# All gates as Strassen sets ahead of a dilated attention without fill

## The chip, the cores and the metric

The kernel runs on one core of a Trainium2 chip. The metric is the device time of one execution in microseconds, as the median of several runs; lower is better. TensorE (PE) multiplies matrices into PSUM, VectorE (DVE), ScalarE (ACT) and GpSimd (POOL) work elementwise, and SyncE (SP) issues most of the DMA transfers. Each engine runs its own queue in order and waits on semaphores of the others.

## What is computed

One encoder layer is applied to a sample of 1024 rows and a prompt of 256 rows with shared weights, all in float32. Cut to what matters here:

```python
h = rmsnorm(x, norm1_g) * (1 + sc1) + sh1
z = einsum('bsd,de->bse', h, w_in)
c_q, c_kv, k_r, qkv_d, gate_a, gate_b = split(z, cuts)
o_a = mla_attention(...)                      # 16 heads, from c_q, c_kv, k_r
...
# dilated attention: 3 groups of 4 heads of 64, (window, dilation) = (128,1), (512,4), (2048,16)
s = einsum('bqhd,bqjhd->bhqj', q_b, k_g) * scale + alibi
lse = logsumexp(s); p = exp(s - lse)
o = einsum('bhqj,bqjhd->bqhd', p, v_g)
...
o_b = sum(softmax(lses over groups) * outs)
merged = sigmoid(gate_a) * (o_a @ p_a) + sigmoid(gate_b) * (o_b @ p_b)
x = x + gt1 * (merged @ w_out)
```

A conv feed-forward block and a last norm follow.

## The kernel before

A float32 product is made of three products of float32r operands: each operand is split into a high part and the rest, and high x high, high x low and low x high are summed in PSUM (`mm3`, line 88, and its generator `mm3_steps`, line 95). T is 1280 columns (sample and prompt), in chunks `CH` of 512, 512 and 256. All activations lie transposed, 128 features by T.

The first 392 us make the normed input `hH`, `hL` and project it. `product_set` (line 290) multiplies two blocks of 128 output features by a Strassen scheme: seven products of 24 matmuls of 320 columns (`product`, line 235) and sums of them on VectorE and GpSimd. The list `psets` holds ten such sets: queries and keys of the dilated attention (`qk_d`), four blocks of gate b (`gb_d`) and four latent blocks (`lt_d`).

Then comes the dilated attention. Six steps (three groups, two pairs of heads) go over ten tiles of 128 query rows each. `queries_keys` loads a pair's queries and keys from `qk_d` (two heads on 128 partitions), copies the high part on ScalarE (line 628) and subtracts on VectorE (line 630); group 2 is not split. `weights` makes the scores (line 890) for two heads in two PSUM banks, a biased minimum on VectorE (line 895) and the exponential on ScalarE (line 900). `outputs` transposes them on PE (line 910), copies them out of PSUM (lines 914, 916, 919), multiplies by the values (line 925) and copies the result (lines 929, 931).

Between these pieces a fill is issued: `filler` runs 13 blocks (one latent block, four of gate b, eight of gate a), each as 72 plain matmuls by `block` and `mm3_steps` (line 99), 19 pieces for every 20 half tiles (`SIDE`). Beside it run `norms` (the latents' norms) and `modulation` (the second half of the adaLN projection, line 770, with its 256 KB weight loads). What is left of the fill after the last step runs together with `merge`, the combination of the second pair. The first pair is combined in the last step. Then `latents`, `ropes`, `values_out` and `branch_b` follow (gate b, the product with `p_b`), and then the latent attention.

The order on each engine is set by a scheduler of the tile framework from the order in which the code issues the work; buffers (`bufs`) bound how far it can run ahead.

## Time and profile before

| | us |
|---|---|
| median of 3 runs (2441.15 to 2444.96) | 2443.45 |
| the profiled execution | 2446.51 |
| its span | 2444.7 |

| stage, us from the start | what runs |
|---|---|
| 0 to 147 | norm, modulation, first values |
| 147 to 392 | ten Strassen sets |
| 392 to 413 | fill, loads of the first step |
| 413 to 698.5 | dilated attention and fill |
| 698.5 to 743 | rest of the fill, second combination |
| 743 to 809 | ropes, branch B |
| after 809 | latent attention, output, feed-forward |

A row of the windows view gives a stretch's length and each engine's busy time in it, with the number of instructions; PEclk is the granted TensorE clock as a share of 2.4 GHz, and the DMA share is the mean busy share of the 16 DMA engines. PE counts as busy from a matmul's start to its modelled end. A timeline row is start, length, engine, line, operation, output <- input and count; PEld is the weight load.

### The profile page before, as it was taken

The numbers are of one execution on the slowest core, as the hardware profiler recorded it, in microseconds if no ns is written. First come the engines' busy times: TensorE is split into PE (matmuls) and PEld (weight loads), VectorE is DVE, ScalarE is ACT, GpSimd is POOL, SyncE is SP. The second block draws the span as 40 slices with busy tenths as digits, with TensorE's granted clock in tenths as the row PEclk, the third lists the DMA queues.
The fourth block names the chain that finished last, engine by engine and source line by source line (L and its number), as shares of the span: only waits on it lengthen the run. The fifth ranks groups of instructions, "written<-read, shape, count | busy, mean of one in ns | idle before, by whom it ended". The sixth has DMA issues, their size and how long they took to land. (4 is left out here: it accounts for less than half of the span.)

```text
span 2444.7 us, 36879 instructions
## 1 busy us (share of the span) xinstructions
PE 2345.5 (96%) x13115; PEld 1990.2 (81%) x13115; DVE 1508.4 (62%) x2526; ACT 1078.3 (44%) x2102; POOL 1033.7 (42%) x758
## 2 busy tenths in 40 slices
PE   7999999999999999999998999989999999999987
PEld 3899997666677777777776788789999999988875
DVE  4743333443458688888897533486655665559678
ACT  4421212554434477777776433353222322343434
POOL 1033331100135166666677441004655565439373
PEclk9999999999999999999999999999999999999998
DMA  7232225567458833333332853332322223177554
GB/s 266 74 115 97 98 82 181 185 196 237 152 156 291 280 86 85 87 86 88 89 109 74 227 178 118 124 121 78 110 95 81 82 95 105 56 267 241 174 185 153
DMA packets 208019, 342.48 MB, mean 140 GB/s; under 512 B 24365, under 2 KB 86686, under 8 KB 207834
## 3 DMA queue, kind: packets, MB, share of 16 engines
q1 hardware_dynamic: 182238, 311.00, 39.7%
q10 hardware_dynamic: 25596, 29.12, 3.4%
q8 instruction: 103, 1.69, 0.3%
q14 instruction: 82, 0.67, 0.1%
HBM read 236.67 MB, written 94.19 MB: 135 GB/s over the span
## 5 line engine op out<-in xcount | busy, mean ns | idle before, releaser
L243 PE MATMUL X<-t,wh 128*128 128x320 f32 x2864 | 537.3, 309 | 6.9 <-ACT ut L1777 6.9
L243 PEld LDWEIGHTS X<-t,wh 128*128 128x128 f32 x2864 | 450.6, 188 | 7.2 <-ACT ut L1777 7.1
L80 POOL TENSOR_TENSOR pl<-p,ph 128x512 fp32r<-128x512 f32 x224 | 298.4, 1342 | 135.4 <-ACT ph L1190 102.0
L243 PE MATMUL X<-t,wl 128*128 128x320 f32 x1432 | 327.1, 310 | 1.9 <-DVE wl L77 1.0
L243 PEld LDWEIGHTS X<-t,wl 128*128 128x128 f32 x1432 | 239.6, 188 | 3.0 <-DVE wl L77 1.6
L1189 ACT ACTIVATE p<-S 128x512 f32<-128x512 f32 x272 | 163.5, 601 | 105.4 <-issue 39.6
L1171 DVE TENSOR_REDUCE m<-mi 128x1 f32<-128x512 f32 x256 | 174.0, 686 | 35.7 <-PE mi L1170 32.8
L229 ACT CAST wh<-wr 128x512 fp32r<-128x512 f32 x113 | 70.2, 622 | 280.7 <-PE X L243 183.2
L99 PE MATMUL pp<-t,wh 128*128 128x512 f32 (+1 forms) x624 | 188.3, 381 | 0.5 <-DVE sm L663 0.5
L77 DVE TENSOR_TENSOR ut<-X,ut 128x640 f32<-128x640 f32 x126 | 101.5, 819 | 130.7 <-PE X L243 78.2
L1190 ACT ACTIVATE ph<-S 128x512 fp32r<-128x512 f32 x272 | 162.6, 598 | 1.2 <-issue 0.4
L1869 PE MATMUL Y<-bh,ah 128*128 128x512 f32 x385 | 151.8, 395 | 8.2 <-DVE ut L77 6.8
L80 POOL TENSOR_TENSOR wl<-R,wh 128x512 fp32r<-128x512 f32 x60 | 96.4, 1607 | 146.0 <-ACT wh L229 146.0
L1869 PE MATMUL Y<-bl,ah 128*128 128x512 f32 x385 | 151.9, 395 | 6.2 <-POOL bl L80 6.2
L1869 PE MATMUL Y<-bh,al 128*128 128x512 f32 x385 | 151.4, 393 | 0.0
L80 POOL TENSOR_TENSOR wl<-wr,wh 128x512 fp32r<-128x512 f32 (+2 forms) x39 | 45.4, 1165 | 247.1 <-ACT wh L208 216.3
L77 DVE TENSOR_TENSOR wl<-wr,wh 128x512 fp32r<-128x512 f32 x128 | 112.8, 883 | 48.1 <-ACT wh L229 41.7
L243 PE MATMUL X<-R,wh 128*128 128x320 f32 x736 | 138.1, 309 | 0.0
L99 PEld LDWEIGHTS pp<-t,wh 128*128 128x128 f32 x624 | 107.4, 192 | 30.4 <-issue 12.7
L77 DVE TENSOR_TENSOR pt<-X,pt 128x640 f32<-128x640 f32 x60 | 48.6, 823 | 134.8 <-PE X L243 83.8
L77 DVE TENSOR_TENSOR al<-ar,ah 128x640 fp32r<-128x640 f32 x75 | 93.6, 1249 | 55.8 <-ACT ah L1843 55.8
L77 DVE TENSOR_TENSOR ac<-ac,p 128x512 f32<-128x512 f32 x160 | 111.0, 694 | 9.2 <-ACT p L1189 7.1
(436 smaller groups left out, 5668.9 us busy)
## 6 DMA issues: line engine op xcount, KB each, us to landing
ac_d<-ut SPq DMA_DIRECT2D x77, 320.0 KB
ar<-ac_d SPq DMA_DIRECT2D x75, 320.0 KB
R<-in_w_up_dram SPq DMA_DIRECT2D x84, 256.0 KB
br<-in_w_down_dram SPq DMA_DIRECT2D x77, 256.0 KB
ad<-in_ada_w_dram SPq DMA_DIRECT2D x64, 256.0 KB
rw<-in_w_in_dram SPq DMA_DIRECT2D x20, 512.0 KB
V<-v_d SPq DMA_DIRECT2D x16, 640.0 KB
v<-in_ada_w_dram SPq DMA_DIRECT2D x32, 256.0 KB
```

What stands on the lines that cost most here:

```text
L77: nc.vector.tensor_tensor(out=out, in0=a, in1=b, op=op)
L80: nc.gpsimd.tensor_tensor(out=out, in0=a, in1=b, op=op)
L99: nc.tensor.matmul(ps, lhsT=w[k], rhs=x[k], start=(k == 0 and w is wh and x is xh), stop=(k == n - 1 and w is wl))
L229: nc.scalar.copy(out=h, in_=a)
L243: nc.tensor.matmul(ps[:, z, 0:320], lhsT=a[:, k, :], rhs=b[q][k][:, 320 * z:320 * z + 320], start=(j == 0 and i == 0), stop=(j == n - 1 an ...
L1171: nc.vector.reduce_max(out=m2[:, i, c:c + 1], in_=ps, axis=AX.X)
L1189: nc.scalar.activation(out=p_, in_=ps, func=AF.Exp, scale=MSCALE)
L1190: nc.scalar.activation(out=ph, in_=ps, func=AF.Exp, scale=MSCALE)
L1869: nc.tensor.matmul(ps, lhsT=a[:, P * j:P * j + P], rhs=b, start=(f == 0 and a is ah and b is bh), stop=(f == HF - 1 and a is al))
```

## The change

All 16 gate blocks are now Strassen sets: `psets` holds the queries and keys, the latents, gate b and gate a, 16 sets. The one latent block left over is made plain after the eighth set by `lone_block`. The fill is gone (`filler`, `block`, `SIDE`), and with it `hH`, `hL`, whose pool is closed ahead of the attention.

A head's keys are now stacked: the high part on partitions 0 to 63, the low part on 64 to 127. The queries stand twice, as high parts and as low parts. So two products of 128 rows a head give all four terms, and group 2 is split as well. Each query and key piece is fetched twice, to both halves. The keys' copy is made on GpSimd.

Scores of a tile lie in one PSUM bank of three for two heads, and are issued two tiles ahead (`AHEAD`), across steps. Results of groups 0 and 1 go to DRAM (`nt_d`) and are read back by `combine`. The second combination is moved behind the attention, beside ropes and latents; branch B begins after it.

```diff
-    GB0 = 4
-    psets += [(B_GB + 2 * i, gb_d[2 * i:2 * i + 2]) for i in range(GB0 // 2)]
     psets += [(B_KV, lt_d[3:5]), (0, lt_d[0:2])]
+    psets += [(B_GB + 2 * i, gb_d[2 * i:2 * i + 2]) for i in range(KD // 2)]
+    psets += [(B_GA + 2 * i, ga_d[2 * i:2 * i + 2]) for i in range(KD // 2)]
+    def lone_block(b, to):
+        w = load_w(wpl, w_in[b], P, 4, WB)
+        xs_ = [X() for _ in range(2)]
+        for c, (c0, n) in enumerate(CH):
+            mm3(xs_[c // 2][:, c % 2, 0:n], *w, [t[:, c0:c0 + n] for t in hH], [t[:, c0:c0 + n] for t in hL])
...
-    w0 = load_w(wpl, w_in[2], P, 4, WB)
+        if i == 7:
+            lone_block(2, lt_d[2])
...
-    VB, SB = 8, 7
+    VB, SB, RB, PPB, AHEAD = 10, 9, 14, 1, 2
+    close_pool(hcm)
...
+        for h in range(2):
+            hs = slice(64 * h, 64 * h + 64)
+            kk, qh, ql = [rtile(F32R) for _ in range(3)]
+            res.append((kk, qh, ql))
+            for w, dh in ((1, kk), (0, qh)):
+                for c, (c0, n) in enumerate(CH):
+                    raw = qkt()[:, 0:n]
+                    for z in range(2):
+                        nc.sync.dma_start(out=raw[64 * z:64 * z + 64], in_=qk_d[g, w, pair, hs, c0:c0 + n])
+                    src = natural(raw, g, c)
+                    if w:
+                        nc.gpsimd.tensor_copy(by_class(dh, g, c), src)
+                    else:
+                        nc.scalar.copy(out=by_class(dh, g, c), in_=src)
+                    if w:
+                        dve_tt(by_class(kk[64:P], g, c), natural(raw[64:P], g, c), by_class(f32(kk[64:P]), g, c), ALU.subtract)
+                    else:
+                        dve_tt(by_class(ql, g, c), src, by_class(f32(qh), g, c), ALU.subtract)
+                    yield
...
-            terms = ((qh, kh), (qh, kl), (ql, kh)) if split else ((qh, kh),)
-            for t, (a, b_) in enumerate(terms):
-                for h in range(2):
-                    hs = slice(64 * h, 64 * h + 64)
-                    nc.tensor.matmul(ps[h][:, 0:wn], lhsT=a[hs, q0:q0 + P], rhs=b_[hs, w0:w0 + wn], start=(t == 0), stop=(t == len(terms) - 1))
+            ps = bank("S", 3)
+            for h, (kk, qh, ql) in enumerate(self.heads):
+                for t, a in enumerate((qh, ql)):
+                    nc.tensor.matmul(ps[:, 256 * h:256 * h + wn], lhsT=a[:, P * i:P * i + P], rhs=kk[:, w0:w0 + wn], start=(t == 0), stop=(t == 1))
...
+                nc.sync.dma_start(out=nt_d[pair, g], in_=self.nt)
...
     merge1 = merge()
-    for j, _ in enumerate(side):
-        if j % 4 == 1 or j < 4:
-            next(merge1, None)
-    run(merge1)
+    next(merge1)
...
     for _ in range(12):
         next(rr, None)
-        next(bb, None)
+        next(merge1, None)
         next(lat, None)
+    run(merge1)
```

PE in the middle of the attention, before (group 1 of the first pair, not its start). `PT` and `O` are the banks of the transposed weights and of the outputs, `pp` is the fill's:

```order
L99 MATMUL pp_4452<-t_135,wl_4289 128x512
L910 MATMUL PT_4500<-t_60,sm_4423 128x128 x4
L99 MATMUL pp_4452<-t_136,wh_4294 128x512
L99 MATMUL pp_4452<-t_144,wh_4294 128x512
L99 MATMUL pp_4452<-t_136,wl_4295 128x512
L99 MATMUL pp_4452<-t_137,wh_4294 128x512
L925 MATMUL O_4507<-sm_4501,v_3698 64x128 x4
L99 MATMUL pp_4452<-t_145,wh_4294 128x512
L99 MATMUL pp_4452<-t_137,wl_4295 128x512
```

The same engine at the change of a step, in the changed kernel:

```order
L913 MATMUL O_6279<-sm_6273,v_5652 64x128 x4
L898 MATMUL PT_6353<-t_60,sm_6267 128x128 x4
L879 MATMUL S_6370<-R_5682,R_5683 128x256
L879 MATMUL S_6370<-R_5682,R_5684 128x256
L879 MATMUL S_6370<-R_5819,R_5820 128x256
L879 MATMUL S_6370<-R_5819,R_5821 128x256
L879 MATMUL S_6415<-R_6102,R_6103 128x256
L879 MATMUL S_6415<-R_6102,R_6104 128x256
L879 MATMUL S_6415<-R_6231,R_6232 128x256
L879 MATMUL S_6415<-R_6231,R_6233 128x256
L770 MATMUL AD_6295<-ad_6296,t_104 32x512
L913 MATMUL O_6319<-sm_6313,v_5652 64x128 x4
```

Fill matmuls stood between the transpositions of a tile and its outputs; now scores of later tiles (the second four are of the next step) and transpositions of a later tile stand there, and here and there a modulation matmul (`AD`).

SP's queue at the end of the Strassen stage, before (`pt` is a set's output, `v` a value tile, `qk` a raw query or key piece):

```order
L560 DMA lt_d<-pt_3455 128x1280
L615 DMA v_3695<-vn_d 64x256
L615 DMA v_3695<-vn_d 128x256
L615 DMA v_3698<-vn_d 128x256 x2
L615 DMA v_3701<-vn_d 128x256 x2
L615 DMA v_3704<-vn_d 128x256 x2
L615 DMA v_3707<-vn_d 64x256
L615 DMA v_3707<-vn_d 128x256
L615 DMA v_3710<-vn_d 128x256
L626 DMA qk_3714<-qk_d 128x512
L626 DMA qk_3718<-qk_d 128x512
L626 DMA qk_3722<-qk_d 128x256
```

And in the changed kernel:

```order
L573 DMA ga_d<-pt_4899 128x1280
L630 DMA v_5128<-vn_d 64x256
L630 DMA v_5128<-vn_d 128x256
L630 DMA v_5131<-vn_d 128x256 x2
L630 DMA v_5134<-vn_d 128x256 x2
L630 DMA v_5137<-vn_d 128x256 x2
L630 DMA v_5140<-vn_d 64x256
L630 DMA v_5140<-vn_d 128x256
L630 DMA v_5143<-vn_d 128x256
L643 DMA qk_5148<-qk_d 64x512 x2
L643 DMA qk_5153<-qk_d 64x512 x2
L643 DMA qk_5158<-qk_d 64x256 x2
```

The queue has the same order, the last set's outputs first; the pieces of queries and keys are halves now, 24 of them for the first step where six stood.

## Rows read from the trace of the kernel before

**Rows 1.** Windows by stage: length, each engine's busy time (instructions), clock, DMA

```profile
core 0: us, PE busy (x) PEld busy (x) DVE busy (x) ACT busy (x) POOL busy (x), PEclk, DMA share, GB/s
147.00:392.00 245.00, 245.00 (x1672) 245.00 (x1672) 83.85 (x109) 49.45 (x81) 86.59 (x67) 1.00 0.26 95
...
392.00:413.00 21.00, 19.32 (x96) 15.23 (x95) 3.88 (x6) 4.39 (x8) 2.57 (x2) 1.00 0.81 267
413.00:698.50 285.50, 275.59 (x1715) 182.92 (x1713) 127.11 (x446) 139.07 (x396) 33.31 (x27) 0.98 0.59 187
698.50:743.00 44.50, 44.20 (x237) 37.99 (x237) 21.61 (x31) 12.51 (x21) 11.54 (x6) 1.00 0.69 209
743.00:809.00 66.00, 61.37 (x325) 52.07 (x325) 55.26 (x98) 31.63 (x68) 36.37 (x30) 0.97 0.91 306
```

**Rows 2.** The same windows, the fill's matmuls (line 99) alone: PE, PEld

```profile
413.00:698.50 285.50, 162.35 (x616) 100.49 (x614) 0.98 0.59 187
698.50:743.00 44.50, 44.09 (x236) 37.96 (x236) 1.00 0.69 209
```

**Rows 3.** Timeline of PE, fill alone: start, length, what, count

```profile
395.92 0.62 PE L99 MATMUL pp<-t,wh 128*128 128x512 f32 x2
396.38 0.39 PE L99 MATMUL pp<-t,wl 128*128 128x512 f32 x1
396.60 0.62 PE L99 MATMUL pp<-t,wh 128*128 128x512 f32 x2
...
403.40 0.40 PE L99 MATMUL pp<-t,wh 128*128 128x256 f32 x2
403.63 0.28 PE L99 MATMUL pp<-t,wl 128*128 128x256 f32 x1
403.75 0.40 PE L99 MATMUL pp<-t,wh 128*128 128x256 f32 x2
```

**Rows 4.** Timeline, the lead-in to the attention

```profile
395.37 7.36 SPq L615 DMA_DIRECT2D v<-vn_d  x11
403.15 1.27 SPq L626 DMA_DIRECT2D qk<-qk_d  x3
...
413.54 0.38 PE L890 MATMUL S<-R,R 64*128 64x256 f32 x2
```

**Rows 5.** DMA issues from 392 to 835: transfer, count, size of each

```profile
qk<-qk_d SPq DMA_DIRECT2D x24, 256.0 KB
...
qk<-qk_d SPq DMA_DIRECT2D x12, 128.0 KB
```

**Rows 6.** Groups of VectorE by form, 392 to 743: busy, mean ns | idle before

```profile
L77 DVE TENSOR_TENSOR R<-qk,R 128x512 fp32r<-128x512 f32 x16 | 15.0, 942 | 6.1 <-ACT R L628 6.1
...
L663 DVE COPY sm<-pp 128x512 f32<-128x512 f32 x13 | 9.0, 689 | 20.5 <-PE pp L99 19.6 <-ACT sm L900 0.9
...
L77 DVE TENSOR_TENSOR wl<-wr,wh 128x512 fp32r<-128x512 f32 x12 | 8.2, 687 | 6.4 <-ACT wh L208 6.3
...
L77 DVE TENSOR_TENSOR R<-qk,R 128x256 fp32r<-128x256 f32 x8 | 4.2, 522 | 4.1 <-ACT R L628 4.1
```

**Rows 7.** Windows of PE beside a fall of the clock, and scores in the timeline

```profile
428.00:431.40 3.40, 1.92 (x21) 1.38 (x20) 0.00 (x0) 2.73 (x9) 1.26 (x1) 1.00 0.66 197
431.40:438.30 6.90, 6.90 (x38) 4.95 (x37) 3.44 (x13) 1.69 (x6) 0.00 (x0) 0.51 0.50 154
...
436.28 1.01 PE L890 MATMUL S<-R,R 64*128 64x256 f32 x6
...
480.89 0.61 PE L890 MATMUL S<-R,R 64*128 64x256 f32 x6
```

**Rows 8.** One tile's instructions: lowest, median, highest ns; and a GpSimd group, 392 to 743

```profile
L77 DVE TENSOR_TENSOR wl<-rw,wh x10: 681/682/1362, 140.2 to 362.5; 128x512 fp32r<-128x512 f32 x10
...
L80 POOL TENSOR_TENSOR sm<-sm,qk 128x512 f32<-128x512 f32 x6 | 7.8, 1302 | 57.4 <-ACT qk L705 23.1 <-DMA qk<-qk_d 11.7 <-ACT sm L705 11.4
```

**Rows 9.** Timeline, first and last piece of the second pair's combination

```profile
697.88 0.27 SPq L956 DMA_DIRECT2D st_d<-sm  x1
...
731.74 1.49 DVE L77 TENSOR_TENSOR R<-R,R 128x1280 fp32r<-128x1280 f32 x1 [1.34 <-ACT R L837]
```

More of the change, by code (lines that the diff above doesn't have):

```diff
@@ L826, in combine @@
         yield
-        n0, n1, n2 = nts[pair]
+        ns = [rtile(), rtile(), nts[pair]]
+        for g in range(2):
+            nc.sync.dma_start(out=ns[g], in_=nt_d[pair, g])
+        n0, n1, n2 = ns
         for g in range(3):
@@ L846, in last_steps @@
         yield from gather(1, rest[0], range(2))
-    rest, LD, SPEED = [], 2, 2
-    side, side2, side3 = filler(), norms(), modulation()
-    values(0)
-    run(queries_keys(0, 0, qk[0, 0]))
-    for _ in range(8):
-        next(side)
-    for pair, g in steps:
-        split = g < 2
-        (qh, ql), (kh, kl) = qk[pair, g]
-        nxt = steps.index((pair, g)) + 1
-        more = queries_keys(*steps[nxt], qk[steps[nxt]]) if nxt < len(steps) else last_steps()
-        if pair and g < 2:
-            values(g + 1, 0, 4)
-        if g == 0:
-            bt = [mk(cpl, [P, 384], tag="bs", bufs=4) for _ in range(2)]
-            for h in range(2):
-                nc.sync.dma_start(out=bt[h], in_=bias0[2 * pair + h])
-            btab = {0: bt, 1: bt}
-        else:
-            w = 384 if g == 1 else P
-            btab = {}
-            for q, src in enumerate((bias1s, bias1p) if g == 1 else (bias2s, bias2p)):
-                if g == 1:
-                    btab[q] = [mk(cpl, [P, 384], tag="bs", bufs=4) for _ in range(2)]
-                else:
-                    both = mk(cpl, [P, 384], tag="bs", bufs=4)
-                    btab[q] = [both[:, P * h:P * h + P] for h in range(2)]
@@ new lines, with __init__ @@
+    rest, LD = [], 2
+    class Step:
+        def __init__(self, n):
+            self.pair, self.g = pair, g = steps[n]
+            self.wide = g < 2
+            self.heads = qk[pair, g]
+            self.nt, self.v = rtile(), vts[g]
+            self.stat = mk(cpl, [P, 40], tag="stat", bufs=2)
+            self.bias = {}
+            for q, src in enumerate(((bias0, bias0), (bias1s, bias1p), (bias2s, bias2p))[g]):
+                if g == 0 and q:
+                    self.bias[1] = self.bias[0]
+                    continue
+                if g < 2:
+                    self.bias[q] = [mk(cpl, [P, 384], tag="bs", bufs=BB) for _ in range(2)]
+                else:
+                    both = mk(cpl, [P, 384], tag="bs", bufs=BB)
+                    self.bias[q] = [both[:, P * h:P * h + P] for h in range(2)]
@@ L876 @@
                 for h in range(2):
[L877 to L890 removed]
+                    nc.sync.dma_start(out=self.bias[q][h][:, 0:384 if g < 2 else P], in_=src[2 * pair + h])
@@ L928, in outputs @@
             if i % 2:
-                nc.scalar.copy(out=cls(nt, g, i), in_=oo)
+                nc.scalar.copy(out=cls(self.nt, self.g, i), in_=oo)
             else:
-                nc.vector.tensor_copy(cls(nt, g, i), oo)
-        quota = 0.0
-        nxt_w = weights(0)
-        for i in range(NT):
-            now, nxt_w = nxt_w, weights(i + 1) if i + 1 < NT else None
-            for part in range(2):
-                quota += SIDE / 20
-                while quota >= 1:
-                    quota -= 1
-                    next(side, None)
-                if part == 0:
-                    outputs(i, *now)
-                if part == 0 or i % 2:
-                    next(side3, None)
-            for _ in range(SPEED if nxt == len(steps) else 1):
-                next(more, None)
-            if steps.index((pair, g)) >= NORM[0]:
-                for _ in range(NORM[1]):
-                    next(side2, None)
@@ new lines @@
+    side2, side3 = norms(), modulation()
+    values(0)
+    run(queries_keys(0, 0, qk[0, 0]))
+    jobs = [(n, i) for n in range(len(steps)) for i in range(NT)]
+    cur, ahead_ = {0: Step(0)}, []
+    for m in range(AHEAD):
+        ahead_.append(cur[0].weights(m))
+    for j, (n, i) in enumerate(jobs):
+        pair, g = steps[n]
+        if i == 0:
+            more = queries_keys(*steps[n + 1], qk[steps[n + 1]]) if n + 1 < len(steps) else last_steps()
+            if pair and g < 2:
+                values(g + 1, 0, 8)
+        if j + AHEAD < len(jobs):
+            n2, i2 = jobs[j + AHEAD]
+            if n2 not in cur:
+                run(more)
+                cur[n2] = Step(n2)
+            ahead_.append(cur[n2].weights(i2))
+        cur[n].outputs(i, *ahead_.pop(0))
+        for _ in range(2):
+            next(more, None)
+        for _ in range(1 + i % 2):
+            next(side3, None)
+        next(side2, None)
+        if i == NT - 1:
+            cur.pop(n).finish()
+            run(more)
+            if pair and g < 2:
+                values(g + 1, 8)
@@ L976 @@
     close_pool(psC)
-    close_pool(hcm)
     lcm = open_pool("lat", "right")
```

109 lines of the change are left out of this document (40 added, 69 removed).

## The prediction

> **What bounds the kernel now.** I read the stage windows first, because the change touches one stretch only. From 147 to 392 us ten Strassen sets run and PE is busy in all 245 us: 1672 matmuls, the other engines at a third, the DMA engines at 0.26 [rows 1]. That stage is bound by the number of matmuls. From 392 to 743 us the dilated attention runs together with a fill: 13 blocks of 72 plain matmuls. PE is busy there too, but two sorts of work make it so: in 413 to 698.5 PE is busy 275.6 us, of which 162.4 us are the fill [rows 1, 2]. Without it PE has only 113 us of attention's own work in 285.5 us. The other resources are what the reader is to see next: in the same window VectorE is busy 127 us, ScalarE 139 us, and the DMA engines 59% of the time; in the next stage, 743 to 809, the DMA engines are at 0.91 and VectorE at 55 of 66 us [rows 1]. So attention is hidden under the fill as much as the fill is hidden in attention, and the stretch after it is close to what the DMA engines give.
>
> I take everything from the last Strassen matmul (392) to the end of branch B (809, the end of the last window of [rows 1]): 417 us now. Behind that nothing is changed but addresses.
>
> **The gates as Strassen sets.** One set is 7 products of 24 matmuls, 168; at 245 us for 1672 [rows 1] that is 24.6 us. Six more sets: 148 us. The latent block that stays plain (72 matmuls) is put between two sets. Plain matmuls run three of 512 columns in 0.68 us and three of 256 in 0.35 us [rows 3], so a block (48 and 24) takes 13.7 us. Together 161 us are added to the Strassen stage, PE-bound as it is; loads, splits and the set's output writes lie beside it as they do now. Removed are 13 blocks of 13.7 us, 178 us of PE time. On PE alone the gates gain 17 us. But the 178 us were not alone on the path: while they ran, attention ran. The new stretch is 161 + A + B, with A for attention without fill and B for what follows it up to the end of branch B. **The change breaks even at A + B = 256 us.**
>
> **A, attention alone.** Four prices.
>
> Lead-in. SP issues the values' loads (11 in 7.4 us from 395.4), then the first query and key pieces at 403.15; the first score matmul is at 413.5 [rows 4]. That is 21 us after the last Strassen matmul, hidden under fill now, uncovered after. In the change the same queue stands behind the last set's two output writes, and the first score of the second head needs about the 20th of 24 half pieces, through five buffers that VectorE frees one by one. At 0.42 us an issue (1.27 us for three [rows 4]) they take 8.4 us where six take 7 now, and casts and subtractions follow one another twice: 21 to 27 us, taken 24.
>
> DMA. Share times length is the time in which all engines would be full: 0.81 x 21 + 0.59 x 285.5 = 185 us for A, 0.69 x 44.5 + 0.91 x 66 = 91 us for B [rows 1]. A megabyte costs 3.0 us (0.91 at 306 GB/s) to 3.2 us (0.59 at 187). Out go the fill's weights and outputs, 1.18 MB a block. 236 of its 936 matmuls stand behind 698.5 [rows 2], so 9.7 blocks leave A (-36 us) and 3.3 leave B (-12 us). In come the duplicated queries and keys: 24 loads of 256 KB and 12 of 128 KB are fetched twice [rows 5], +7.9 MB, +24 us. Four results are written to DRAM and read back, 640 KB each, +12 us in A and +4 us in B. A needs 186 us of full DMA, B 83 us: **269 us, already over the 256 us of break-even.** Full use is not reached: the best long window has 0.91. With 12 us of it moved in the lead-in, A = 24 + 174 / 0.9 = 217 us.
>
> VectorE. 131 us busy in A now [rows 1]. The key and query splits go from 24 subtractions to 72: 32 more of 0.942 us and 16 more of 0.522 us, 38 us. One evacuation and one weight split a block leave, 0.69 us each, 13 us [rows 6]. That makes 156 us, 70% of 222 us: not the bound, but every score waits for it.
>
> PE. Scores go from six matmuls of 64 rows, which took 0.61 us [rows 7], to four of 128 rows; at 0.117 us each and the drain this is the same. The casts of the keys on GpSimd are new: 36, nearest row 1.30 us (a two-input operation of the same size [rows 8]), at most 47 us; between nothing and twice that it stays free beside them, since it is busy 36 us there now [rows 1], and I cost it at nothing. The clock is a price of its own. In 428 to 431.4 PE had attention's matmuls alone, was busy 1.92 of 3.4 us, and the next 6.9 us ran at a granted clock of 0.51 (1.2 GHz): six scores took 1.01 us in place of 0.61 [rows 7]. All of A looks like that window. The Trainium skill ("TensorE: Matmul & The Clock Gate", the section on why this matters for your kernels) says that gaps between bursts of matmuls send the array back to half clock; the trace agrees. PE's 113 us become up to 226 us at half clock, which would make A 24 + 226 = 250 us. I expect both levels by turns, mostly beside DMA waits, and add 5 us: **A = 222 us**, bounds 199 (DMA at 0.97 after a lead-in of 21) and 260 (half clock and some waits).
>
> **B, after attention.** 110.5 us now (698.5 to 809). The fill's last 44 us are gone, but they covered the combination of the second head pair: from its statistics' write (697.9) to its last subtraction (733.2) it took 35 us [rows 9], and branch B's products cannot start before. They then take 144 matmuls with 60 of the value projection between, about 35 us of PE by [rows 3]; the rope and latent projections fill the first 35 us. So at least 70 us by this chain, 83 / 0.9 = 92 us by the DMA engines, and VectorE's 77 us (22 + 55 [rows 1]) lie in between. Taken 95, bounds 84 and 105.
>
> **Sum.** 161 + 222 + 95 = 478 us where 417 stand: +61 us. The profiled execution took 2446.5 us (span 2444.7), 3 us over the median 2443.45; 2446.5 + 61 - 3 = **2505 us**, slower by 2.5%.
>
> **Rivals.**
> 1. Half clock and queues taking turns. PE is in order, each transposition waits for an exponential and each output for a copy; nothing else is left to issue. A = 250 to 260, B = 100 to 105: 511 to 526, time 2538 to 2552. For it: the window of [rows 7]. Against it: look-ahead of two tiles across steps, so that transpositions of one tile stand before the outputs of the one ahead. 16%.
> 2. GpSimd and VectorE collide. The 128x512 subtraction that takes 0.682 us took 1.362 us at worst in the Strassen stage, where GpSimd works too [rows 8]. 36 casts stand beside 72 such subtractions; if all double, VectorE goes from 156 to about 212 us, and A = 24 + 202 / 0.9 = 248, time 2531. "GPSIMD Engine Reference" of the Trainium skill (Specifications) says that GpSimd shares its SBUF interfaces with VectorE's two-input operations, which speaks against this placing; by it the sum would be 2531, by the row's median 2505. Casts fill a fifth of A, so the full price is unlikely. 6%.
> 3. Well packed. DMA at 0.97 throughout, full clock: A = 199, B = 84: 444 us, +27, time 2470. 10%.
> 4. Faster. The one way: VectorE's queue is never empty and the DMA engines turn out to have room. A = 24 + 146 (VectorE's 156 less 10 in the lead-in) = 170, B = 76: 407 us, -10, time 2433. It decides for faster once A + B is under 251. Against it: the 269 us of DMA would have to fit into 246, unless the share counts time in which a packet only waits. 7%, and 4% for a time within 0.2% (about what a measurement here tells from no change).
>
> **Chances and range.** My forecast (2480 to 2530) has 57%. Faster 7%, same 4%, slower 89%. The range 2460 to 2550 holds it and rivals 2 and 3, leaves out faster and same (11%) and the edges of rival 1 and of my own sum, some 20% in all.
>
> **What would show it.** In the profile after: the Strassen stage ends near 392 + 161 = 553 us with PE still full; then PE idles for 20 us or more before the first score; attention ends 200 to 240 us after the last Strassen matmul, with DMA at 0.8 or more, VectorE at about 70% and PE at about half, the granted clock clearly under 0.98; branch B ends 85 to 105 us behind it. I am wrong if the attention stretch is under 190 us, if DMA is well below 0.75 in it (then something else is the bound), or if the stages behind 809 move.

## The result and the profile after

The changed kernel takes **2623.08 us** (2614.30 to 2625.38 in four runs) beside 2444.2 us for the kernel before on the same chip: a ratio of 1.0729, interval 1.0699 to 1.0760. It is slower by 179 us where 61 us were predicted. The profiled execution took 2624.36 us, span 2622.6 us.

The windows by stage (length, busy time of each engine with its instructions, granted clock, DMA share, GB/s) answer to [rows 1]:

```profile
core 0: us, PE busy (x) PEld busy (x) DVE busy (x) ACT busy (x) POOL busy (x), PEclk, DMA share, GB/s
147.00:553.00 406.00, 406.00 (x2747) 404.02 (x2746) 134.10 (x175) 81.78 (x133) 142.71 (x111) 1.00 0.27 94
553.00:587.00 34.00, 9.74 (x45) 8.41 (x45) 10.74 (x27) 8.88 (x21) 6.71 (x10) 0.56 0.71 220
587.00:700.00 113.00, 94.34 (x527) 50.61 (x525) 65.00 (x195) 58.56 (x165) 23.30 (x25) 0.86 0.66 204
700.00:820.00 120.00, 79.61 (x358) 38.37 (x358) 58.39 (x171) 41.01 (x126) 15.09 (x14) 0.71 0.67 209
820.00:848.00 28.00, 23.35 (x112) 13.84 (x110) 14.27 (x70) 13.25 (x55) 4.47 (x7) 0.62 0.22 63
848.00:880.00 32.00, 2.87 (x5) 1.07 (x4) 16.94 (x39) 4.73 (x8) 7.78 (x3) 0.50 0.46 121
880.00:990.00 110.00, 74.14 (x323) 60.04 (x323) 65.14 (x104) 34.74 (x69) 44.57 (x31) 0.79 0.74 242
```

The Strassen stage is what was predicted, full to 553. Attention then runs to 848 and branch B ends at 989. The stages behind keep their length: 2622.6 - 989 = 1634 us, before 2444.7 - 809 = 1636 us. So the whole loss lies in A and B: against the prediction A is 71 us longer and B 46 us. The reader is to see what is *not* there: between 587 and 820 no engine is busy for more than 84% of a window (PE, at a granted clock of 0.86 and 0.71), VectorE for 58% and then 49%, and the DMA engines stand at 0.66. Nothing is full, and yet it takes 233 us. Share times length of the DMA engines over the four windows of A is 185 us, where the prediction has 186 us; only the time in which they do it is not 217 but 293 us.

When no engine is full, the next view is the waits. The longest in 554 to 848 (engine and line, what it waited for, total us, times, longest):

```profile
POOL R L646 <- DMA qk<-qk_d: 142.1, 26, 37.0
ACT R L648 <- DMA qk<-qk_d: 47.6, 10, 15.2
POOL sm L80 <- ACT qk L705: 44.6, 9, 7.7
ACT sm L888 <- DVE stat L883: 42.7, 26, 10.4
DVE R L77 <- POOL R L646: 42.2, 17, 11.7
ACT R L917 <- PE O L913: 40.9, 23, 3.5
PEld AD L770 <- DMA ad<-in_ada_w_dram: 37.9, 14, 6.1
PE AD L770 <- DMA ad<-in_ada_w_dram: 27.8, 10, 5.2
```

Every engine waits for another, and at the head of the list stand loads: pieces of keys and queries (L643 issues them, L646 and L648 cast them) and the modulation's weights (AD). All of them are issued by SP, in order. SP's issues add up to 172 us of A's 293 us (370 transfers), of which the halved pieces alone are 80 us; its own waits add 119 us. The longest of these:

```profile
SPq L734 <- DVE qk L733: 21.6, 11, 5.3
SPq L764 <- PE AD L770: 18.1, 9, 6.8
SPq L643 <- DVE R L77: 13.8, 14, 2.9
```

L734 writes the norms' results, L764 loads the modulation's weights into a ring of four buffers, L643 loads the pieces into a ring of five. So SP issues or waits nearly all the time. That alone proves nothing: in the kernel before it did so too, with 117 us of issues and 181 us of waits in the 306 us from the last set to the last result. What a microsecond on SP is worth, the experiments have to say. The issues by line, as lowest, median and highest ns:

```profile
L643 SPq DMA_DIRECT2D qk<-qk_d x144: 444/587/1235, 563.3 to 811.4; - x144
...
L764 SPq DMA_DIRECT2D ad<-in_ada_w_dram x64: 327/382/1255, 582.1 to 816.7; - x64
```

The lead-in, answering to [rows 4], from the timeline:

```profile
557.17 6.06 SPq L630 DMA_DIRECT2D v<-vn_d  x11
...
570.99 1.73 PE L879 MATMUL S<-R,R 128*128 128x256 f32 x6 [16.13 <-ACT R L648]
578.66 1.73 PE L879 MATMUL S<-R,R 128*128 128x256 f32 x6 [5.93 <-ACT R L648]
...
586.79 0.69 PE L913 MATMUL O<-sm,v 64*64 64x128 f32 x4
```

The first score comes 16 us after the last set. The first score of the second head, for which PE waits 5.9 us at the cast of that head's first query piece, comes 24 us after it, and the first output 32 us after it (30 us in the kernel before).

### The profile page after: what moved, and what is told of

Read it like the earlier page. It is cut to its first block, busy times and chain, and to the rows that moved or that the text cites. A ratio compares the mean times of both kernels' runs of the same rounds, so it can differ in the third digit from the quotient of the medians.

```text
span 2622.6 us, 37406 instructions
## 1 busy us (share of the span) xinstructions
PE 2392.8 (91%) x13179; PEld 2034.9 (78%) x13179; DVE 1572.9 (60%) x2615; ACT 1082.7 (41%) x2102; POOL 1102.2 (42%) x824
## 5 line engine op out<-in xcount | busy, mean ns | idle before, releaser
L244 PE MATMUL X<-t,wh 128*128 128x320 f32 x3536 | 663.5, 309 | 6.8 <-ACT ut L1778 6.8
L244 PEld LDWEIGHTS X<-t,wh 128*128 128x128 f32 x3536 | 556.5, 188 | 7.2 <-ACT ut L1778 7.1
L244 PE MATMUL X<-t,wl 128*128 128x320 f32 x1768 | 403.3, 309 | 1.7 <-POOL wl L80 1.0
L244 PEld LDWEIGHTS X<-t,wl 128*128 128x128 f32 x1768 | 295.9, 188 | 2.5 <-POOL wl L80 1.2
L230 ACT CAST wh<-wr 128x512 fp32r<-128x512 f32 x131 | 81.4, 621 | 329.7 <-PE X L244 228.5
L77 DVE TENSOR_TENSOR pt<-X,pt 128x640 f32<-128x640 f32 x96 | 77.7, 823 | 217.2 <-PE X L244 137.8
L80 POOL TENSOR_TENSOR wl<-rw,wh 128x512 fp32r<-128x512 f32 x48 | 61.9, 1289 | 143.8 <-ACT wh L230 143.8
L244 PEld LDWEIGHTS X<-R,wh 128*128 128x128 f32 x736 | 115.5, 188 | 0.3 <-ACT ut L1725 0.3
L230 ACT CAST wh<-rw 128x512 fp32r<-128x512 f32 x64 | 39.8, 621 | 179.8 <-PE X L244 165.1
```

The costliest lines, as they stand in the source:

```text
L77: nc.vector.tensor_tensor(out=out, in0=a, in1=b, op=op)
L80: nc.gpsimd.tensor_tensor(out=out, in0=a, in1=b, op=op)
L230: nc.scalar.copy(out=h, in_=a)
L244: nc.tensor.matmul(ps[:, z, 0:320], lhsT=a[:, k, :], rhs=b[q][k][:, 320 * z:320 * z + 320], start=(j == 0 and i == 0), stop=(j == n - 1 an ...
```

## The experiments

Each kernel is read by the same three marks: the last Strassen product, the last copy of an attention result (A lies between them), and the last write of branch B (B). The stages behind took 1626 to 1637 us in all of them. "SP" is the number of transfers that SP issued in A and the time of the issues; MB is what was moved in A. Each of these kernels but the changed one was run once. Two of them (e7 and e8) leave the attention as it is in the changed kernel and have A = 286 and 288 where that has 293: read differences of A under 8 us as none, and a gain against the 293 us as up to 7 us smaller.

| kernel | time us | A | B | SP issues | MB in A |
|---|---|---|---|---|---|
| changed kernel | 2623.1 | 293 | 141 | 370, 172 us | 57 |
| e1_one_issue | 2830.2 | 505 | 142 | 298, 367 us | 57 |
| e2_no_modulation | 2622.2 | 238 | 200 | 306, 145 us | 40 |
| e3_old_scores | 2575.3 | 239 | 143 | 258, 106 us | 49 |
| e4_idle_products | 2624.7 | 302 | 135 | 380, 174 us | 58 |
| e5_stacked_in_dram | 2589.5 | 260 | 141 | 298, 112 us | 57 |
| e6_ring_of_twelve | 2609.1 | 284 | 135 | 365, 172 us | 56 |
| e7_issues_added | 2619.4 | 286 | 142 | 370, 172 us | 57 |
| e8_combine_later | 2621.2 | 288 | 143 | 370, 172 us | 57 |
| c1_modulation_ahead | 2590.8 | 274 | 130 | 366, 170 us | 56 |
| c2_issues_in_place | 2645.5 | 320 | 133 | 509, 212 us | 56 |
| c3_loads_eased | 2563.1 | 239 | 130 | 294, 115 us | 56 |
| c4_combine_on_act | 2598.4 | 303 | 106 | 346, 166 us | 62 |
| d1_four_ahead | 2565.5 | 245 | 134 | 293, 115 us | 56 |
| d2_no_norms | 2554.8 | 175 | 189 | 225, 88 us | 44 |
| n1_norms_ahead | 2545.8 | 223 | 130 | 294, 120 us | 56 |
| f1_eased_and_act | 2547.4 | 252 | 103 | 272, 114 us | 62 |

(The expectations give A to the last minimum in places, which is 4 to 5 us less.)

The theories, by their numbers in the expectations: 1, SP's issues and in-order waits pace the attention; 2, PE's own chain at a low clock; 3, the DMA engines' bytes; 5, the ring of five piece buffers; 7, the waits at the modulation's loads; 8 and 9, a block's own chain against queues filled with side work; 10 and 11, the norms' loads against the norms' chain (4 and 6 stand in no run). A diff is cut to its main lines and is against the changed kernel; those of d1, d2 and n1 are against c3, that of the last two kernels against the kernel before.

**Is it PE and its clock?**

```
+        idle, kk = pp(), cur[n].heads[0][0]
+        for _ in range(5):
+            nc.tensor.matmul(idle, lhsT=kk[:, 0:P], rhs=kk[:, 0:512], start=True, stop=True)
```

> The changed kernel with five products of 128x512 that nobody reads behind each of the 60 blocks of outputs (300 in all, 64 us at full clock), which take the place that the fill had on PE. Theory 1 (SP's queue): PE's busy share and its granted clock rise, the attention keeps its length, 285 to 300 us, total 2615 to 2635. Theory 2 (the half clock lengthens PE's own chain): the clock near 0.95 takes back 40 us or more of its 205 us of busy time, attention below 270 us, total below 2600.

The window 587 to 820, first of the changed kernel, then of this one:

```profile
587.00:820.00 233.00, 173.95 (x884) 88.98 (x883) 123.39 (x365) 99.58 (x290) 38.39 (x39) 0.79 0.66 206
```

```profile
587.00:820.00 233.00, 203.49 (x1098) 118.11 (x1098) 124.23 (x356) 99.41 (x285) 38.03 (x38) 0.92 0.65 203
```

PE does 214 more products, the clock goes from 0.79 to 0.92, and every other engine does the same work in the same time; the total moves by 1.6 us, and A is 302 where 293 stood. The gain of 40 us or more that theory 2 asked for did not come, though a matmul of the scores takes 317 ns in the mean in place of 370. The run does not price the clock by itself, because the added products stand in PE's queue too and could hide a gain. But in c1 and e2 below A is 19 and 55 us shorter at a *lower* clock, 0.71 and 0.63 over A for 0.74: the low clock is not what makes A long. What it costs by itself stays open.

**Is it the issues on SP?** Four kernels.

```
-                    for z in range(2):
-                        nc.sync.dma_start(out=raw[64 * z:64 * z + 64], in_=qk_d[g, w, pair, hs, c0:c0 + n])
+                    nc.sync.dma_start(out=raw, in_=qk_d[g, w, pair, hs, c0:c0 + n].partition_broadcast(2))
```

> The changed kernel, but each piece of the keys and queries is loaded by one DMA that reads the 64 rows twice, in place of two DMAs of 64 rows: 72 issues fewer on SP, the same bytes. Theory 1 (the in-order queue of SP, busy with 175 us of issues and about 100 us of waits in the 292 us of the attention, paces it): 72 issues of 0.56 us fall away, the attention ends about 40 us earlier, total 2575 to 2595. Theory 2 (the PE's own chain at a clock of 0.6 to 0.9 paces it): within 8 us of 2623. Theory 3 (the DMA engines are full for transfers of this shape, though their mean share is 0.65): the bytes and packets are the same, so within 8 us of 2623.

This did not test what it was meant to, and all three expectations missed. The issue of one such transfer took 660 ns in the median and up to 6199, SP's issues fill 367 us of A, and the transfers themselves became slow: A 505 us with the DMA engines at a share of 0.35 in 587 to 1020. The Trainium skill ("DMA: Bandwidth & Descriptors", the section on why a DMA increments its semaphore by 16) says that the number of DMA engines which share a transfer is the largest number up to 16 that divides the slowest dimension of both access patterns. The source's slowest dimension is 2 here, so two engines would carry it; the low share agrees, but no row shows the engines one by one. As a test of theory 1 the run says nothing, since it changes the issue and the transfer at once.

```
+                        nc.sync.dma_start(out=no_d[noop[0]:noop[0] + 1], in_=vecT[0:1, 0:16])
```

> The changed kernel with one more DMA of 64 bytes behind each of the 144 loads of keys and queries, which nobody waits for: the cost of an issue on SP alone, doubled in number. Issues of such small transfers took 0.27 to 0.33 us on SP. Theory 1 (SP's issues pace the attention): 144 x 0.3 = 43 us more, attention 325 to 345 us, total 2655 to 2675. Theories 3 and 5 (DMA bytes, ring): under 10 us more, total 2620 to 2635.

Void: the scheduler issued all 144 between 49 and 153 us, since they hung on nothing; A holds the same 370 issues as the changed kernel. It serves as the second measurement of an unchanged attention.

```
-                    for z in range(2):
-                        nc.sync.dma_start(out=raw[64 * z:64 * z + 64], in_=qk_d[g, w, pair, hs, c0:c0 + n])
+                    nc.sync.dma_start(out=raw, in_=q2_d[g, w, pair, h, :, c0:c0 + n])
...
+                for h in range(2):
+                    for r in range(2):
+                        nc.sync.dma_start(out=q2_d[i // 2, i % 2, z, h, 64 * r:64 * r + 64], in_=flat(out[z])[64 * h:64 * h + 64])
```

> The changed kernel, but the Strassen stage writes every head's 64 rows of keys and queries twice, one copy below the other, into a tensor of its own (48 writes of 64 rows in place of 12 of 128, in a stage where the DMA engines are at 0.25), and the attention loads each piece of 128 rows by one plain DMA: 72 issues in place of 144, the same bytes in transfers of the kind that the kernel before had. Theory 1 (SP's issues and in-order waits pace the attention): 80 us of issues become 25 to 30, attention 235 to 250 us in place of 293, total 2565 to 2585. Theory 3 (the DMA engines and their bytes pace it) and theory 5 (the ring of five piece buffers and the round trip of a piece pace it): within 10 us of 293, total 2613 to 2633.

```
                         nc.sync.dma_start(out=raw[64 * z:64 * z + 64], in_=qk_d[g, w, pair, hs, c0:c0 + n])
+                        nc.sync.dma_start(out=wide[z:z + 1, 512:520], in_=qk_d[g, w, pair, 0:1, c0:c0 + 8])
```

> The changed kernel with one more DMA of 32 bytes behind each of the 144 half loads of keys and queries, into columns of the same buffer that nobody reads: in the run before this one the added transfers hung on nothing and were all issued in the first 153 us, so they tested nothing; here they are tied to the buffer and stand among the loads. 144 issues of about 0.25 us are 36 us more on SP. Theory 1 (SP's issues pace the attention; 53 us of them fewer had shortened it by 32): 22 to 40 us longer, attention 310 to 330 us, total 2640 to 2662. Theory 3 and 7 (bytes, modulation): under 10 us longer.

The loads of the pieces in e5, and the added transfers in c2 (lowest, median, highest ns):

```profile
L648 SPq DMA_DIRECT2D qk<-q_d x72: 319/382/825, 564.5 to 777.2; - x72
```

```profile
L646 SPq DMA_DIRECT2D qk<-qk_d x144: 228/435/992, 550.7 to 837.8; - x144
```

With the same 57 MB, 59 us of issues fewer shorten A by 34 us, somewhat less than theory 1 asked for; 40 us of issues more, with 4.6 KB moved by them, lengthen it by 26 us, as theory 1 expected. Both ways a microsecond of issue on SP is worth about 0.6 us of A (0.57 and 0.66; 0.5 and 0.8 if the 287 us of e7 and e8 are taken for the unchanged attention). Theory 3, the DMA engines' bytes, is out as the bound, since they are the same in all three (56 MB in c2). Theory 1 holds, though not alone. Neither run changes the issue time and nothing else: in e5 a piece is also one transfer in place of two, and in c2 the added transfer has to land before its buffer is used again. The same page of the Trainium skill ("DMA: Bandwidth & Descriptors", the section that issuing engines are not separate DMA queues) calls the time to initiate a DMA usually small beside the DMA. Here it is not: the 144 halves take 80 us to issue, and their 15.7 MB are some 51 us of all 16 engines (an estimate, by 185 us for the 57 MB of A).

**Is it the ring of buffers, the modulation, the old or the new scores?**

```
-                    raw = qkt()[:, 0:n]
+                    raw = mk(qxcm[1], [P, 512], tag="qx", bufs=12)[:, 0:n]
```

> The changed kernel, but the pieces of keys and queries have a ring of their own of 12 buffers in place of sharing five with the norms. Theory 5 (a piece can be loaded only when the fifth before it has been cast and subtracted): attention 250 to 270 us in place of 293. Theory 1 (SP's issues): SP's waits at this line (13.8 us) can leave, the issues stay, 278 to 293 us. Theory 3 (DMA bytes): 285 to 295 us.

A = 284, beside 286 to 293 for an unchanged attention and the 250 to 270 that theory 5 asked for: theory 5 is out.

```
-        for _ in range(1 + i % 2):
-            next(side3, None)
```

> The changed kernel, but the modulation's steps (64 loads of 256 KB, their products, copies and transposes) are not stepped within the attention and run in one piece behind it. Read by stages: the attention, 293 us in the changed kernel. Theory 1 (SP's queue): the 64 issues of 0.45 us and the 18 us that the queue stood at these loads leave it, attention 240 to 250 us. Theory 2 (PE's chain and clock): 28 us of waits of the modulation's products leave, the clock falls further, 265 to 300 us. Theory 3 (DMA bytes): 16.8 of some 50 MB leave, attention 195 to 215 us. In every theory the loads come back behind the attention with 55 to 85 us, so that the total is above 2600.

```
+        for _ in range(7):
+            load()
         for c in range(4, 12):
...
-                w = ad_tile()
-                nc.sync.dma_start(out=w, in_=ada_w[k * P:(k + 1) * P, 512 * c:512 * c + 512])
-                ws.append(w)
+                load()
```

> The changed kernel, but the modulation's loads run seven ahead of its products through a ring of twelve buffers, in place of four loads with the four products right behind the fourth; bytes and issues are the same. Theory 7 (PE, in order, stands at the modulation's loads for the 38 and 28 us that the trace shows, with the attention's products behind them and no fill to do): attention 240 to 262 us in place of 289. Theory 1 (SP's issues pace it): 280 to 292 us, total above 2612. The run without modulation took 233 us; what this kernel leaves above that is the price of its bytes and issues.

Without the modulation A falls by 55 us, more than theory 1 and less than theory 3 asked for; the loads come back behind it and the total is the same. With its loads only issued earlier, A falls by 19 us (12 to 14 against e7 and e8) and B by 11, between what theories 7 and 1 asked for. So the 38 and 28 us of waits at line 770 are worth less than they read.

```
-            kk, qh, ql = [rtile(F32R) for _ in range(3)]
+            dh, dl = (rtile(F32R), rtile(F32R)) if split else (rtile(), None)
...
+            terms = ((qh, kh), (qh, kl), (ql, kh)) if self.wide else ((qh, kh),)
```

> One part of the change alone: the gates are Strassen sets ahead of an attention without fill, as in the changed kernel, but keys and queries are loaded whole (36 issues in place of 144), split as before and scored with three products over 64 rows for each head (two heads at a time; the third step with one product in full fp32, as before). Theory 1 (SP's queue): 108 issues of 0.56 us and the longer lead-in (12 us) leave, attention 215 to 235 us in place of 293, total 2540 to 2565. Theory 2 (PE's chain and clock): more products in each score, and as few others: attention 285 to 320 us, total 2615 to 2650. Theory 3 (DMA): the key and query bytes halve (9.8 MB fewer of 50), attention 235 to 250 us.

The stacked scores, with all that they bring, cost 54 us of A in this place (47 to 48 against e7 and e8), and the Strassen gates with the fill gone cost the rest: 2575 is still 133 us above the kernel before. PE does more, as the three-product scores ask for (1105 matmuls for 1025), and A is shorter all the same. Which of the other things makes it so the run does not tell: 112 issues and 8 MB fewer, but also 38 us of VectorE and 33 us of GpSimd.

**What sets the floor at 238?** Three kernels meet there, with 40 to 56 MB and 106 to 145 us of issues.

> Three changes to the loads together: keys and queries written twice in the Strassen stage and loaded by one plain DMA a piece, with a ring of their own of 12 buffers, and the modulation's loads seven ahead of its products. The same bytes, 72 issues fewer. If issues, ring and modulation are what held the attention (32 + 8 + some 30 us): 215 to 230 us, the 222 us of the prediction, total 2535 to 2560. If another chain (a block's own scores, exponentials, transpositions and outputs, two tiles ahead) is close behind, as the run without modulation (233 us) and the one with the old scores (235 us) could mean: 233 to 250 us, total 2560 to 2580.

c3 joins the edits of e5, e6 and c1. A = 239: 55 us of the 71 over the prediction are gone, less than the parts by themselves (34, 10 and 19 us), and a third kernel stands at this floor.

```
-    VB, SB, RB, PPB, AHEAD = 10, 9, 14, 1, 2
+    VB, SB, RB, PPB, AHEAD = 10, 9, 14, 1, 4
...
-            sb = stile()
+            sb = mk(qxcm[1], [P, 512], tag="sb", bufs=6)
```

> The run with the three eased loads (236 us of attention), with scores four tiles ahead of their outputs in place of two (a ring of six buffers of their own for them; the pieces' ring 8 and the modulation's 10, five loads ahead). Theory 8 (a block's own chain of scores, minimum, exponential, transposition, copy, output sets the floor of 235 us, since PE and ScalarE stand at it in order): deeper look-ahead hides it, attention 200 to 222 us, total 2528 to 2552. Theory 9 (the floor is VectorE's and GpSimd's in-order work, splits and norms among it, whatever PE has ready): 230 to 242 us, total 2557 to 2570.

```
-        next(side2, None)
         if i == NT - 1:
```

> The run with the three eased loads (236 us), but the norms' steps (squares, sums, scaling, rope of the shared key: 29 loads, 15 writes and some 80 operations on VectorE, ScalarE and GpSimd) are not stepped within the attention and run in one piece behind it. Read by stages: theory 8 (the block's own chain) keeps the attention at 228 to 240 us; theory 9 (in-order queues into which the norms' waits are put) shortens it to 195 to 220 us. The norms come back behind it with 30 to 60 us in either case.

A from end to end in c3 and in d2:

```profile
557.00:796.00 239.00, 168.92 (x1024) 107.27 (x1024) 152.43 (x472) 121.45 (x367) 48.93 (x54) 0.76 0.70 234
```

```profile
556.00:731.00 175.00, 149.61 (x982) 89.18 (x982) 132.64 (x429) 107.78 (x344) 36.87 (x41) 0.87 0.72 251
```

Deeper look-ahead does nothing (245, with somewhat smaller rings for the loads), so theory 8 is out. Taking the norms out takes 64 us out of A, more than either theory asked for, though the work that leaves is 20 us of VectorE, 14 us of ScalarE and 12 us of GpSimd, side by side. As long as they last, one step of the norms stands behind each block, on the same in-order queues; while it waits, the block behind it waits too. VectorE is now at 76% and PE at 85%, where they had 64% and 71%. The norms come back in B, so nothing is won in total but 8 us.

```
+                fetch()
-                r = qkt()[:, 0:n]
-                nc.sync.dma_start(out=r, in_=lt_d[b0 + j, :, c0:c0 + n])
+                r = rs.pop(0)
```

> The run with the three eased loads (236 us of attention; here with rings of 8 and 10 for pieces and modulation), and the norms' latents loaded four steps ahead into a ring of six buffers of their own, in place of a load with its reader right behind it. Same work, same bytes. Without the norms the attention took 171 us. Theory 10 (VectorE, ScalarE and SP stand in order at the norms' loads, 20 to 26 us on VectorE and 10 to 15 on ScalarE, and every block of the attention behind them): 195 to 216 us, total 2515 to 2545. Theory 11 (the chain from ScalarE over GpSimd and PE to VectorE and back to SP inside the norms holds the queues, whenever the loads come): 224 to 240 us, total 2548 to 2570.

A from end to end:

```profile
554.00:777.00 223.00, 169.12 (x1023) 102.34 (x1023) 151.30 (x469) 120.62 (x367) 49.80 (x54) 0.80 0.75 251
```

A = 223, total 2545.8: 15 of the 64 us were waits at the norms' loads. The result lies between the two expectations, a little outside that of theory 10 and just under that of theory 11. What part of the other 49 us is their own work, the 12 MB and 28 us of issues they bring, and what their chain of engines, stays open.

**B, behind the attention.** In the kernel before, the last step of the attention lasted 37.8 us (from the 50th to the 60th result copy) and the first pair's combination had its weights written at 677.7 us, 21 us *ahead* of the attention's end; only the second pair's [rows 9] stood behind it. Without fill the last step lasts 20.1 us. SP and ScalarE then (timeline):

```profile
853.65 1.19 SPq L823 DMA_DIRECT2D wt_d<-bs  x4
...
859.24 7.41 SPq L798 DMA_DIRECT2D ld<-st_d  x8
866.69 0.28 SPq L931 DMA_DIRECT2D st_d<-sm  x1
...
882.97 1.50 SPq L823 DMA_DIRECT2D wt_d<-bs  x4
```

```profile
871.30 1.26 ACT L838 CAST R<-R 128x1280 fp32r<-128x1280 f32 x1 [20.64 <-DVE R L77]
872.46 0.61 ACT L993 CAST t<-v 128x512 fp32r<-128x512 f32 x1
```

The first pair's weights are written 5 us *after* the attention's end (848.3), the second pair's statistics leave at 866.7, behind the gathers on SP, and the second weights at 883. Two combinations follow one another in the open where one was predicted.

```
-            (dve_tt if g == 2 else pool_tt)(ns[g], ns[g], wb, ALU.mult)
-            yield
+        tails.append((pair, ns, wbs))
...
+    combined(*tails.pop(0))
```

> The changed kernel, but the multiplications, sums and casts that end each combination are moved behind the first latent loads and copies (the first pair) and behind the weights of the second (the second pair), and all loads of a combination are issued before its first multiplication; nothing in the attention is touched. Read by stages: attention to the last product of branch B, 141 us in the changed kernel. If the cast of the first combination, at which ACT stood 20.6 us with the latents' copies behind it, held the stage up: 115 to 128 us, total 2597 to 2612. If the chain of the two combinations itself (loads, multiplications on GpSimd, sums) sets the start of branch B: 135 to 145 us, total 2617 to 2628.

No change in B (143): the cast at which ScalarE stood 20.6 us, which looks like the culprit in the rows, does not hold the stage up by itself. The wait did not leave either. ScalarE now stands 21.2 us at the load of `p_b`, which SP issues at 862.7, behind the same gathers.

```
-                        nc.sync.dma_start(out=d[nb * h:nb * h + nb].rearrange("b (r i) -> b r i", r=r_),
+                        nc.scalar.dma_start(out=d[nb * h:nb * h + nb].rearrange("b (r i) -> b r i", r=r_),
...
-            nc.sync.dma_start(out=st_d[pair, g].rearrange("s h (i q) -> (s h i) q", q=P), in_=srow)
+            nc.scalar.dma_start(out=st_d[pair, g].rearrange("s h (i q) -> (s h i) q", q=P), in_=srow)
```

> The changed kernel, but all transfers of the two combinations (statistics out and in, weights, first two results) are issued by ScalarE's queue in place of SP's, and the statistics' second step has eight buffers in place of two. In the changed kernel the last statistics were ready at 847 us and their write was issued at 866.7, since SP stood at the first combination's gathers. If that order on SP makes the two combinations follow one another: from the attention's end to the end of branch B 120 to 130 us in place of 145, total 2600 to 2612. If the work of the combinations on GpSimd and VectorE sets it: 138 to 148 us, total 2613 to 2628. Against it: ScalarE's exponentials stand behind the issues in the last step, which can lengthen the attention by 5 us.

B falls by 35 us to 106, total 2598.4. But the last step of the attention grows from 20 to 42 us, since the exponentials now stand behind issues that wait (ScalarE, 800 to 860: 9.4, 5.5, 3.6 and 2.7 us at the combination's pieces). So 22 of the 35 us only change places; the other 12 us of the total gain of 25 lie in the steps before, which is little above the scatter. c4 also gives the statistics eight buffers in place of two; f1, next, does without that and shortens B as well, so it is SP's queue that made the second combination late.

> The run with eased loads and the norms' loads ahead, and with it the two combinations' transfers on ScalarE's queue (the run that shortened the changed kernel by 26 us). If the gains add up, theory 10: 2490 to 2520; theory 11: 2522 to 2545. In either case above the 2442 of the kernel before, because the Strassen stage alone costs 161 us and the break-even of attention and rest is 256 us.

f1 joins n1 and c4. The gains do not add up, against both expectations: 2547.4 where n1 has 2545.8. B is 28 us shorter than n1's and A 29 us longer, 24 of them in the last step (43.6 for 19.4 us). Here the queue that issues the first combination only decides where the time shows, in the last step or behind it.

**Was the fill worth its place?** The kernel before, with one and two sets more and the fill thinner.

```
-    GB0 = 4
+    GB0 = 6
...
-    SIDE = 19
+    SIDE = 15
```

> The kernel before with one Strassen set more (six of branch B's gate blocks in place of four), eleven blocks left as fill and the fill's pace set to 15 in place of 19. Nothing else of the change. A set is 24.6 us, two blocks of fill are 27.4 us of PE. As long as PE bounds the attention (its floor without fill was 235 us with these scores, it takes 306 with the fill): 2 to 8 us faster than before, ratio 0.997 to 0.999. If the fill hides time that another chain needs anyway: 5 to 20 us slower, ratio 1.002 to 1.008.

(8 and 11 in the other.)

> The kernel before with two Strassen sets more (all eight of branch B's gate blocks), nine blocks left as fill and the fill's pace set to 11. Sets 49.2 us, four blocks of fill 54.8 us of PE. If PE bounds the attention still (306 less 55 is 251 us, above the floor of 235): 4 to 12 us faster than before, ratio 0.995 to 0.998. If waits that the fill covered come up as it gets thinner: 5 to 25 us slower, ratio 1.002 to 1.010.

g6 takes 2456.72 us (four runs), ratio 1.0058 (1.0043 to 1.0074); g8 2447.53 us (ten runs), ratio 1.0026 (1.0011 to 1.0040). Both intervals lie above 1, so each is a little slower than the kernel before, and by far less than the whole change. From the last Strassen product to the end of branch B the kernel before needs 417 us, g6 399, g8 370. The first set costs 25 us and gives back 18, both cost 50 and give back 47, where 27 and 55 us of PE work left. So four of the 13 blocks of fill still give back most of their time, and the loss of the whole change must come with the blocks that leave after them and with the scores. That it loses more with one set than with two I cannot explain; the pace of the fill was set by hand in both.

## Why the prediction was wrong

The direction was right, and the size was not: 179 us for 61 us, outside the range. Of the 118 us between them 71 lie in A and 46 in B. By its steps:

- **Strassen stage, +161 us: right.** The last product ends at 554.9 where 392.7 stood; the lone block and the six sets cost what their matmuls cost.
- **Break-even A + B = 256 us: right** as an account. A + B is 434 us, and 162 + 434 - 417 = 179 us is the whole difference.
- **Lead-in 24 us: right in its sum.** The first score of the second head comes at 578.7, 24 us after the last set. A price in it was too low: the halves stood at 0.42 us an issue, from a row of 128-row pieces, and the first 24 took 15.1 us, 0.63 each. That the sum is right all the same is in part luck.
- **DMA, A needs 186 us of full use: right (185). That the engines would be full at 0.9: the step that failed.** 174 / 0.9 and 5 us for the clock make 198 us behind the lead-in; it took 270. The 0.9 came from the best long window of the kernel before [rows 1], 743 to 809, which is another stage: there transfers of mostly 128 to 256 KB were issued by two queues, SP's and ScalarE's, at shares of 0.59 and 0.32. In A it is 0.63, in c3 0.70, and with the norms' loads eased too (n1) 0.75. A transfer in A is issued when SP has got past everything ahead of it, among it writes that wait for VectorE and loads that wait for a buffer. The prediction treated SP as free behind the lead-in: 144 halves for 36 pieces, at a price per byte and not per issue. Priced at what they took, they are 80 us on a queue that issued for 117 us of A before, 15 us of it for the 36 pieces.
- **VectorE 156 us, 70%: the work right (147 us up to the last minimum), the share not**, since the stretch was longer (50%). The subtractions took 1.0 us in the mean, near the 0.942 of [rows 6]; rival 2, in which they double, did not come.
- **Half clock, +5 us: not shown.** The clock is at 0.5 to 0.86. In e4 more clock with more products brought nothing, and c1 and e2 are shorter at a lower clock, so the 71 us are not its doing; its own price was not measured. Rival 1 asked for 28 to 38 us from queues that take turns, with PE's as the one that counts. Queues do wait for one another here; the runs put the sizes that they could measure to SP's queue and to the side work.
- **GpSimd's casts at nothing: right for GpSimd, not for those who wait.** They took 33 us of it, but VectorE waited 42 us for them, and GpSimd itself 142 us for their pieces.
- **Norms and modulation were costed at nothing**, as unchanged parts. They were hidden by the fill, and the fill left: c1, n1 and d2 show 19, 15 and up to 64 us. This is the omission that mattered most beside SP's issues.
- **B = 95 us: wrong, 141.** The prediction counted one combination in the open; with a last step of 20 us for 38 there are two. They stand in SP's queue one behind the other, and c4, which takes them out of it, shortens B by 35 us and lengthens the last step by 22. The share of the DMA engines in B makes 96 us of full use where 83 were counted, and their mean share is 0.68, not 0.9.
- The prediction's own sign for error ("if DMA is well below 0.75 in it (then something else is the bound)") is what the windows show. With eased loads and norms (n1) A is 223 us, the 222 of the prediction, but at a DMA share of 0.75: the agreement of the number is luck, not its reason.

What is shown: the ring of five and look-ahead do not set A, nor do the bytes by themselves; issues on SP and the waits at the modulation's and norms' loads do, in the sizes above. Of the 71 us over the prediction, c3 and n1 take back 70. What stays open is what the clock costs by itself, the split of the 49 us that the norms still cost, and why B stays at 130 to 143 us in all kernels that neither move work behind the attention nor take the combinations off SP's queue.

## What to carry over

Before a filler is taken out, list everything else that it hid, the unchanged side work too: such steps have waits in queues that work in order, and these waits show once the filler is gone. Price DMA loads by the issue as well as by the byte, at the shape they will have, on the queue that issues them; a DMA share from another stage, with other transfers on two issuing queues, is no forecast for a stage whose loads wait for buffers in one. And a step that hides another must still be as long as what it hides when the change has shortened it.

## What the runs showed of the hardware

- The issue of a piece on SP took 0.38 us in the median on 128 partitions (e5) and 0.587 us on 64 in the changed kernel; the same half took 0.45 us in c2, where a transfer of 32 bytes stood behind each. So two halves cost two to three times the whole, and the price is not one of shape alone.
- One DMA that reads its rows twice by a stride of zero is no substitute: 0.66 us to issue, up to 6.2, and A went from 293 to 505 us.
- Three hundred products that nobody reads raised the granted clock from 0.79 to 0.92 in 587 to 820 us and took a matmul of the scores from 370 to 317 ns in the mean, and A did not get shorter (302 for 293 us).
